# Matmul with layer norm: later row tiles of A loaded one at a time, four rows to a partition

## The chip, the cores and the metric

The kernel runs on one core of a Trainium2 chip. The metric is the device time of one execution in microseconds, and lower is better. The engines are TensorE (PE in the profile), VectorE (DVE), ScalarE (ACT), GpSimd (POOL) and SyncE (SP). SyncE, ScalarE and GpSimd also issue DMA transfers, each on a queue of its own.

## The reference

```python
m, k, n = 2048, 2048, 2048        # a: m x k, b: k x n, all float32
x = np.matmul(a, b)
mean = np.mean(x, axis=-1, keepdims=True)
var = np.var(x, axis=-1, keepdims=True)
normalized = (x - mean) / np.sqrt(var + eps)
return (gamma * normalized + beta).astype(np.float32)
```

## The kernel before

A has 16 row tiles of 128 rows (`i` or `g`), the contraction has 16 slices of 128 (`t` or `kt`), and the output has 4 column blocks of 512 (`q`), one PSUM bank each; there are 8 banks. B is loaded in 32 pieces of 512 KB, `w{kt}_{h}` with `h` 0 for the left 1024 columns and 1 for the right, through 8 buffers (`bigp`), and cast to fp16 into `b16`, where all of it stays. Each piece is cast half by VectorE and half by ScalarE (`cast_left`, `cast_right`). A matmul needs A transposed, `at[i]`, with the contraction in the partitions. The order of every engine's instructions is the order in which the code is written; each engine works through its own list, and semaphores between them are set by the tiles that they share.

The program has these stages:

- Tiles 0 to 3 of A are loaded by the sixteen `f` loads, cast by VectorE and transposed by TensorE. Tiles 0 to 3 are multiplied with B in four phases: left half with slices 0 to 7, right half with slices 0 to 7 (their sums are put by in SBUF), left half with slices 8 to 15, right half with slices 8 to 15. At the end of each of the last two phases `add_up` adds the sum put by and so frees the bank, and `stats` takes row statistics.
- Tiles 4 to 15 then run one after the other, each with all of B: 4 blocks of 16 matmuls. During tile `i` VectorE takes the statistics of its blocks, transposes tile `i + 2`, and normalises tile `i - 1` and, up to tile 11, a half of one of the tiles 0 to 3. `centre` is the first step of `normalise`; it reads the bank, and behind it the bank can be used by the second tile after.
- Tile 15 is normalised by three engines at the end (`normalise_last`).

The later tiles of A, 4 to 15, are loaded in pieces of 512 KB named `p`, through 4 buffers (`firstp`, shared with the `f` loads). A load is four DMAs, one for each group `q` of 32 partitions. ScalarE casts the piece to fp16 (6 buffers, `a16p`). VectorE's transpose then turns blocks of 32 by 32, each within 32 partitions. So the group `q` of 32 partitions has to hold the contraction columns that `at` wants in those partitions, and the four groups come from four places of the contraction. Contraction column `512 c + 128 q + 4 s + t` goes to partition `32 q + s`, slice `4 c + t`, in A as in B.

Before the change a piece `p{i}_{c}` belongs to a pair of tiles, `i` and `i + 1`: partition `32 q + r` holds the rows `r`, `32 + r`, ... of both tiles (eight rows) with one quarter `c` of the contraction. Its first four rows are tile `i`, its last four tile `i + 1`. All four pieces are needed for the first of the two tiles. The pieces of the pair 4, 5 are issued on SyncE's queue, one after each second load of B's last eight; the other pairs on GpSimd's queue:

```python
for t in range(KH, n_kt):
    load_b(t, 1)
    if t % 2:
        load_pair(4, (t - KH) // 2, nc.sync)
```

SyncE's queue ends its inputs with gamma and beta, broadcast to all partitions. The outputs follow on it.

Of the kernel before, what the change touches and what calls it, by code (L numbers as in the profile page):

```python
# [9 lines left out]
FP32 = mybir.dt.float32  # L10
FP16 = mybir.dt.float16
# [4 lines left out]
def kernel(  # L16
# [9 lines left out]
    nc = tc.nc  # L26
    P = 128
    M, K = a.shape
    _, N = b.shape
    n_mt = M // P  # L30
    n_kt = K // P
# [8 lines left out]
    firstp = ctx.enter_context(tc.tile_pool(name="firstp", bufs=4))  # L40
    first16 = ctx.enter_context(tc.tile_pool(name="first16", bufs=2))
    a16p = ctx.enter_context(tc.tile_pool(name="a16p", bufs=6))
# [11 lines left out]
    b16 = bpool.tile([P, n_kt, N], FP16)  # L54

    b_rows = b.rearrange("(c p t) n -> c t p n", p=P, t=4)
    a_pieces = a.rearrange("(s r) (c q k) -> q c r s k", r=32, c=4, q=4)

    bnst, x_of, mv_of, rs_of, at = {}, {}, {}, {}, {}
    a_in, b_in, t_of, pair_in, part = {}, {}, {}, {}, {}  # L60

    def load_b(kt, h, queue=None):
        w = bigp.tile([P, NH], FP32, tag="big", name=f"w{kt}_{h}")
# [8 lines left out]
    def cast_right(kt):  # L72
        w = b_in.pop((kt, 1))
        nc.vector.tensor_copy(b16[:, kt, NH:NH + NB], w[:, 0:NB])  # L74
        nc.scalar.copy(b16[:, kt, NH + NB:N], w[:, NB:NH])
# [3 lines left out]
    def load_first(n):  # L79
        g, c = pieces[n]  # L80
        f = firstp.tile([P, 4 * P], FP32, tag="first", name=f"f{g}_{c}")
        nc.sync.dma_start(f, a[ts(g, P), ts(c, 4 * P)])
        a_in[n] = f
# [12 lines left out]
        g, c = pieces[n]  # L96
        nc.vector.tensor_copy(at[g][:, ds(4 * c, 4), :], t_of[n])

    def load_pair(i, c, queue):
        f = firstp.tile([P, 8, P], FP32, tag="first", name=f"p{i}_{c}")  # L100
        for q in range(4):
            queue.dma_start(f[ds(32 * q, 32)], a_pieces[q, c][:, ds(4 * i, 8)])  # L102
        pair_in[i, c] = f

    def cast_pair(i, c):
        h = a16p.tile([P, 8, P], FP16, tag="a16", name=f"a{i}_{c}")
        nc.scalar.copy(h, pair_in.pop((i, c)))  # L107
        a_in["pair", i, c] = h[:, 0:4]
        a_in["pair", i + 1, c] = h[:, 4:8]

    def new_at(i):
        at[i] = atp.tile([P, n_kt, P], FP16, tag="at", name=f"at{i}")

    def transpose_part(i, c):
        nc.vector.transpose(
            at[i][:, ds(4 * c, 4), :].rearrange("p t (j r) -> p j t r", r=32),
            a_in["pair", i, c].rearrange("p j (k t) -> p j t k", t=4),
        )

    def bank(i, q):  # L120
# [8 lines left out]
    def stats(i, q):  # L129
        if i not in bnst:  # L130
            bnst[i] = stat.tile([P, n_nb, 6], FP32, tag="bnst", name=f"bnst{i}")
        nc.vector.bn_stats(bnst[i][:, q, :], x_of[i, q])
# [78 lines left out]
    with tc.manual_schedule(engines=order):  # L211
        nc.vector.memset(warm, 0.0)  # L212
        nc.vector.memset(ident, 0.0)
        nc.vector.memset(eps_t, float(eps))
        w_ps = psum.tile([P, NB], FP32, tag="c_ps", bufs=8, name="w_ps")

        def warm_up(n):
            for _ in range(n):
                nc.tensor.matmul(w_ps, warm[:, 0:P], warm, start=True, stop=True)  # L219

        nc.gpsimd.affine_select(
            out=ident, in_=ident, compare_op=AluOp.not_equal, fill=1.0,
            base=0, pattern=[[-1, P]], channel_multiplier=1,
        )
        KH = n_kt // 2
        load_first(0)
        load_b(0, 0, nc.scalar)
        load_first(1)
        for n in range(1, KH):
            load_first(n + 1)  # L230
            load_b(n, 0)
        for t in range(KH):
            load_b(t, 1)
            if KH + t + 1 < n_kt:
                load_first(KH + t + 1)
        for t in range(KH, n_kt):
            load_b(t, 0)
        for t in range(KH, n_kt):
            load_b(t, 1)
            if t % 2:  # L240
                load_pair(4, (t - KH) // 2, nc.sync)
        nc.sync.dma_start(gamma_b, gamma.unsqueeze(0).to_broadcast([P, N]))
        nc.sync.dma_start(beta_b, beta.unsqueeze(0).to_broadcast([P, N]))
        for i in range(6, n_mt, 2):
            for c in range(4):
                load_pair(i, c, nc.gpsimd)

        left = [(g, q) for g in range(G) for q in (0, 1)]
        right = [(g, q) for g in range(G) for q in (2, 3)]
        early, late = left[:-1], left[-1]  # L250
        for g in range(G):
            new_at(g)

        warm_up(10)
        cast_first(0)
        turn_first(0)
        cast_first(1)
        warm_up(2)
        for n in range(KH):
            g, c = pieces[n]  # L260
            keep_first(n)
            cast_left(n)
            cast_first(n + 2)
            if n + 1 < KH:
                turn_first(n + 1)
            if n in (0, 1, 2):
                warm_up((3, 3, 2)[n])
            if c == 0:
                for x in early:
                    if x[0] == g:  # L270
                        bank(*x)
            if n == KH - 1:
                break
            for t in range(g + 1):
                for gg, q in early:
                    if gg <= g and (gg == g or t == g):
                        mm(gg, q, 4 * c + t, 0, KH)
        bank(*late)
        cast_right(0)
        for g, q in early:  # L280
            for t in range(4 if g == 3 else KH - 1, KH):
                mm(g, q, t, 0, KH)
            put_by(g, q)
            if (g, q) == (1, 1):
                cast_right(1)
        for t in range(KH):
            mm(*late, t, 0, KH)
        cast_right(2)
        put_by(*late)

        early, late = right[:-1], right[-1]
        for g, q in early:
            bank(g, q)
        for t in range(KH):
            n = KH + t
            turn_first(n)
            if t > 2:
                cast_right(t)
            keep_first(n)
            if n + 2 < n_kt:  # L300
                cast_first(n + 2)
            if t < KH - 2:
                for g, q in early:
                    mm(g, q, t, 0, KH)
        bank(*late)
        for t in range(KH, KH + 2):
            cast_left(t)
        for g, q in early:
            for t in (KH - 2, KH - 1):
                mm(g, q, t, 0, KH)  # L310
            put_by(g, q)
        for t in range(KH):
            mm(*late, t, 0, KH)
        put_by(*late)
        for t in range(KH + 2, n_kt):
            cast_left(t)

        for g, q in left:
            bank(g, q)
        for t in range(KH, KH + 3):  # L320
            for g, q in left:
                mm(g, q, t, KH)
        for j, (g, q) in enumerate(left):
            for t in range(KH + 3, n_kt):
                mm(g, q, t, KH)
            add_up(g, q)
            if j % 3 == 2:
                cast_right(KH + j // 3)

        for g, q in right:  # L330
            bank(g, q)
        new_at(4)
        for c in range(4):
            for t in (KH + 2 * c, KH + 2 * c + 1):
                if t > KH + 1:
                    cast_right(t)
            for g, q in left[4 * c:4 * c + 4]:
                stats(g, q)
            cast_pair(4, c)
            if c < 3:  # L340
                transpose_part(4, c)
        for t in range(KH, n_kt - 2):
            for g, q in right:
                mm(g, q, t, KH)
        for j, (g, q) in enumerate(right):
            for t in (n_kt - 2, n_kt - 1):
                mm(g, q, t, KH)
            add_up(g, q)
            if j == 2:
                transpose_part(4, 3)  # L350
        for g, q in right:
            stats(g, q)
        new_at(5)
        for c in range(4):
            transpose_part(5, c)
            cast_pair(6, c)

        for i in range(G, n_mt):
            if i > G:
                normalise(i - 1)  # L360
            if i + 2 < n_mt:
                new_at(i + 2)
            for q in range(n_nb):
                bank(i, q)
                for t in range(n_kt):
                    mm(i, q, t)
                stats(i, q)
                if i + 2 < n_mt:
                    transpose_part(i + 2, q)
                if i % 2 and i + 3 < n_mt:  # L370
                    cast_pair(i + 3, q)
                if q == 3 and i < 3 * G:
                    normalise((i - G) // 2, (i - G) % 2)
        normalise_last(n_mt - 1)
# [31 lines left out]
```

## Time and profile before

| | us |
|---|---|
| median of 6 runs | 261.87 |
| lowest, highest | 258.91, 264.14 |
| the profiled execution, its own time | 263.12 |
| its span, first to last instruction | 261.3 |
| TensorE busy in the span | 236.9 (91%) |
| VectorE busy | 193.6 (74%) |
| ScalarE busy | 59.0 (23%) |
| GpSimd busy | 49.5 (19%) |

The profile is of one execution. Its own time is 1.8 us longer than the span, since it also holds what lies before the first and behind the last instruction. All times within the trace count from the start of the span. In a timeline a row is: start, duration, engine, line, operation, output and inputs, count, and in brackets how long the engine had been idle and what ended that. A matmul's duration is modelled and overlaps the next one's; the distance of two starts is what it costs. `q` behind an engine's name means its queue: `SPq` is SyncE issuing DMAs. Buffer numbers are left out of names there, so `p_1_196` is a piece `p{i}_1`, and `ps_2_781` a bank of block 2.

### The profile page before, as it was taken

What the parts mean: (1) busy time and instruction counts of PE and PEld (TensorE: products, weight loads), DVE (VectorE), ACT (ScalarE), POOL (GpSimd) and SP (SyncE); (2) the same over time, 40 slices, a digit from 0 to 9 for tenths busy, and PEclk for the clock granted to TensorE, in tenths of its full rate; (3) what the DMA queues carried; (4) which work ended last, traced back from release to release, by engine and by line L of the source; (5) the groups of instructions that cost most, each with busy time, mean ns of one, the idle gap of its engine ahead of it and who ended that gap; (6) DMA issues with size and microseconds to landing.
All of it is one profiled execution on the core that took longest, in us unless ns stands there. A gap on an engine that the chain in (4) does not pass through costs nothing.

```text
span 261.3 us, 3106 instructions
## 1 busy us (share of the span) xinstructions
PE 236.9 (91%) x1108; PEld 107.0 (41%) x1108; DVE 193.6 (74%) x354; ACT 59.0 (23%) x91; POOL 49.5 (19%) x87
## 2 busy tenths in 40 slices
PE   7998989998618999999999999999999999999950
PEld 2454444443202444444444444444444444444420
DVE  1663454379215997999899989999999988665553
ACT  2235617533224150330033003300330000000010
POOL 0000000003313582770055203730000000000003
PEclk9999999999995999999999999999999999999995
DMA  6999999999999765796159712983142303030304
GB/s 203 401 382 404 383 351 413 290 223 244 253 241 278 170 164 106 235 278 224 70 199 268 258 80 110 301 233 161 80 163 82 161 14 149 0 161 0 161 0 161
DMA packets 20303, 52.62 MB, mean 201 GB/s; under 512 B 2881, under 2 KB 6977, under 8 KB 20033
## 3 DMA queue, kind: packets, MB, share of 16 engines
q1 hardware_dynamic: 16160, 41.16, 45.8%
q0 software_dynamic: 3840, 10.49, 17.1%
q10 hardware_dynamic: 288, 0.79, 0.9%
q8 instruction: 8, 0.13, 0.2%
q14 instruction: 7, 0.05, 0.1%
HBM read 35.65 MB, written 16.78 MB: 201 GB/s over the span
## 4 chain that ended last, share of the span: by engine, by line
PE 67%; DMA 26%; DVE 3%; issue 1%; SPq 1%; ACT 0%; ACTq 0%; DVEq 0%
DMA w_1_212<-in_b_dram 5%; DMA p_0_187<-in_a_dram 4%; DMA w_0_173<-in_b_dram 4%; DMA w_1_145<-in_b_dram 4%; DMA p_1_196<-in_a_dram 3%; DMA f_1_129<-in_a_dram 3%; DMA f_0_113<-in_a_dram 3%; PE ps_3_2189 L124 1%; PE ps_0_2134 L124 1%; PE ps_1_2058 L124 1%; PE ps_2_1979 L124 1%; PE ps_3_1898 L124 1%; PE ps_0_1840 L124 1%; PE ps_1_1746 L124 1%; PE ps_2_1649 L124 1%; PE ps_3_1558 L124 1%
## 5 line engine op out<-in xcount | busy, mean ns | idle before, releaser
L197 POOL TENSOR_TENSOR y_last<-y_last,gamma_b 128x512 f32<-128x512 f32 x1 | 1.3, 1266 | 81.9 <-ACT y_last L196 81.9
L102 POOL DMA_DIRECT2D p_0_221<-in_a_dram x4 | 2.5, 626 | 57.3 <-DMA p_1_196<-in_a_dram 57.3
L124 PEld LDWEIGHTS <-at_321 128*128 128x128 f16 x64 | 6.0, 99 | 17.6 <-issue 12.9
L124 PE MATMUL ps_2_781<-b_93,at_321 128*128 128x512 f16 x8 | 3.4, 430 | 9.6 <-DVE b_93 L74 9.6
L124 PEld LDWEIGHTS <-at_323 128*128 128x128 f16 x64 | 6.4, 101 | 8.4 <-issue 1.8
L124 PEld LDWEIGHTS <-at_324 128*128 128x128 f16 x64 | 6.4, 100 | 8.3 <-issue 1.6
L124 PEld LDWEIGHTS <-at_322 128*128 128x128 f16 x64 | 6.4, 101 | 8.0 <-issue 1.1
L124 PEld LDWEIGHTS <-at_919 128*128 128x128 f16 x64 | 6.3, 98 | 7.5
L124 PEld LDWEIGHTS <-at_1033 128*128 128x128 f16 x64 | 6.3, 98 | 7.5
L124 PEld LDWEIGHTS <-at_1379 128*128 128x128 f16 x64 | 6.3, 98 | 7.5
L124 PEld LDWEIGHTS <-at_1493 128*128 128x128 f16 x64 | 6.3, 98 | 7.5
L124 PEld LDWEIGHTS <-at_1839 128*128 128x128 f16 x64 | 6.3, 98 | 7.5
L124 PEld LDWEIGHTS <-at_1939 128*128 128x128 f16 x64 | 6.3, 98 | 7.5
L124 PEld LDWEIGHTS <-at_1263 128*128 128x128 f16 x64 | 6.3, 98 | 7.5
L124 PEld LDWEIGHTS <-at_1723 128*128 128x128 f16 x64 | 6.3, 98 | 7.5
L124 PEld LDWEIGHTS <-at_906 128*128 128x128 f16 x64 | 6.3, 98 | 7.5
L124 PEld LDWEIGHTS <-at_789 128*128 128x128 f16 x64 | 6.2, 97 | 7.6
L124 PEld LDWEIGHTS <-at_1149 128*128 128x128 f16 x64 | 6.2, 97 | 7.6
L124 PEld LDWEIGHTS <-at_1609 128*128 128x128 f16 x64 | 6.2, 97 | 7.6
L219 PE MATMUL w_ps<-warm 128*128 128x512 f16 x20 | 7.3, 505 | 1.2 <-DVE warm L212 1.2
L102 POOL DMA_DIRECT2D p_0_281<-in_a_dram x4 | 2.3, 584 | 15.9 <-ACT a_0_1284 L107 15.9
L102 POOL DMA_DIRECT2D p_0_301<-in_a_dram x4 | 2.3, 584 | 15.5 <-ACT a_0_1514 L107 15.5
(580 smaller groups left out, 593.0 us busy)
## 6 DMA issues: line engine op xcount, KB each, us to landing
gamma_b<-in_gamma_dram SPq DMA_DIRECT2D x1, 1024.0 KB, 14.5
beta_b<-in_beta_dram SPq DMA_DIRECT2D x1, 1024.0 KB, 16.0
w_0_105<-in_b_dram ACTq DMA_DIRECT2D x1, 512.0 KB, 5.2
w_0_111<-in_b_dram SPq DMA_DIRECT2D x1, 512.0 KB, 7.0
w_0_115<-in_b_dram SPq DMA_DIRECT2D x1, 512.0 KB, 7.8
w_0_119<-in_b_dram SPq DMA_DIRECT2D x1, 512.0 KB, 6.4
w_0_123<-in_b_dram SPq DMA_DIRECT2D x1, 512.0 KB, 7.0
w_0_127<-in_b_dram SPq DMA_DIRECT2D x1, 512.0 KB, 7.8
```

Source lines behind the costliest of these rows:

```text
L102: queue.dma_start(f[ds(32 * q, 32)], a_pieces[q, c][:, ds(4 * i, 8)])
L124: nc.tensor.matmul(x_of[i, q], at[i][:, kt, :], b16[:, kt, ds(q * NB, NB)], start=(kt == lo), stop=(kt == hi - 1),)
L197: nc.gpsimd.tensor_tensor(y, y, gamma_b[:, q3], AluOp.mult)
L219: nc.tensor.matmul(w_ps, warm[:, 0:P], warm, start=True, stop=True)
```

## The change

A piece `p{i}_{h}` now belongs to one tile and one half `h` of its rows. Partition `32 q + r` holds the four consecutive rows `4 r` to `4 r + 3` of the tile, two of them in each half, with all four quarters of the contraction. The size is the same, 512 KB, and so are the four DMAs of 32 partitions and their runs of 512 bytes; a tile needs two pieces. A transpose now takes row `j` of each partition with the whole contraction, 16 slices by 32 rows, and writes every fourth column of `at[i]`, from column `j` on. Before, it took four rows of a partition with four slices and wrote all columns of these.

```diff
-    a_pieces = a.rearrange("(s r) (c q k) -> q c r s k", r=32, c=4, q=4)
+    a_pieces = a.rearrange("(i r j) (c q k) -> q i r (j c) k", r=32, j=4, c=4, q=4)
...
-    def load_pair(i, c, queue):
-        f = firstp.tile([P, 8, P], FP32, tag="first", name=f"p{i}_{c}")
+    def load_tile(i, h, queue):
+        f = firstp.tile([P, 8, P], FP32, tag="first", name=f"p{i}_{h}")
         for q in range(4):
-            queue.dma_start(f[ds(32 * q, 32)], a_pieces[q, c][:, ds(4 * i, 8)])
-        pair_in[i, c] = f
-
-    def cast_pair(i, c):
-        h = a16p.tile([P, 8, P], FP16, tag="a16", name=f"a{i}_{c}")
-        nc.scalar.copy(h, pair_in.pop((i, c)))
-        a_in["pair", i, c] = h[:, 0:4]
-        a_in["pair", i + 1, c] = h[:, 4:8]
+            queue.dma_start(f[ds(32 * q, 32)], a_pieces[q, i][:, ds(8 * h, 8)])
+        tile_in[i, h] = f
+
+    def cast_tile(i, h):
+        a16 = a16p.tile([P, 2, 4, P], FP16, tag="a16", name=f"a{i}_{h}")
+        nc.scalar.copy(a16.rearrange("p j c k -> p (j c) k"), tile_in.pop((i, h)))
+        tile_in[i, h] = a16
...
-    def transpose_part(i, c):
+    def transpose_part(i, j):
         nc.vector.transpose(
-            at[i][:, ds(4 * c, 4), :].rearrange("p t (j r) -> p j t r", r=32),
-            a_in["pair", i, c].rearrange("p j (k t) -> p j t k", t=4),
+            at[i].rearrange("p ct (r j) -> p j ct r", j=4)[:, j],
+            tile_in[i, j // 2][:, j % 2].rearrange("p c (k t) -> p c t k", t=4),
         )
...
-            if t % 2:
-                load_pair(4, (t - KH) // 2, nc.sync)
+        for i in (4, 5):
+            for h in (0, 1):
+                load_tile(i, h, nc.sync)
...
-        for i in range(6, n_mt, 2):
-            for c in range(4):
-                load_pair(i, c, nc.gpsimd)
+        for i in range(6, n_mt):
+            for h in (0, 1):
+                load_tile(i, h, nc.gpsimd)
```

The hand-written order around the change moves with it: the casts of B's right half now stand between the add-ups of the left half and between its statistics, tile 4's casts and transposes stand behind all of them, and from tile 6 on each tile's two casts stand in the loop of the tile two before it, where the four casts of a pair stood in every second tile's loop.

On SyncE's queue, in B's last eight right halves and what follows (`w{kt}_1` is a right half of B, `p4_0` the first piece of tile 4, or of the pair 4 and 5), there stood before:

```order
L64 DMA w9_1_185<-in_b_dram 128x1024
L102 DMA p4_0_187<-in_a_dram 32x8x128 x4
L64 DMA w10_1_192<-in_b_dram 128x1024
L64 DMA w11_1_194<-in_b_dram 128x1024
L102 DMA p4_1_196<-in_a_dram 32x8x128 x4
L64 DMA w12_1_201<-in_b_dram 128x1024
L64 DMA w13_1_203<-in_b_dram 128x1024
L102 DMA p4_2_205<-in_a_dram 32x8x128 x4
L64 DMA w14_1_210<-in_b_dram 128x1024
L64 DMA w15_1_212<-in_b_dram 128x1024
L102 DMA p4_3_214<-in_a_dram 32x8x128 x4
L242 DMA gamma_b_88<-in_gamma_dram 128x2048
```

and in the changed kernel, in the same place:

```order
L64 DMA w10_1_187<-in_b_dram 128x1024
L64 DMA w11_1_189<-in_b_dram 128x1024
L64 DMA w12_1_191<-in_b_dram 128x1024
L64 DMA w13_1_193<-in_b_dram 128x1024
L64 DMA w14_1_195<-in_b_dram 128x1024
L64 DMA w15_1_197<-in_b_dram 128x1024
L102 DMA p4_0_199<-in_a_dram 32x8x128 x4
L102 DMA p4_1_204<-in_a_dram 32x8x128 x4
L102 DMA p5_0_209<-in_a_dram 32x8x128 x4
L102 DMA p5_1_214<-in_a_dram 32x8x128 x4
L242 DMA gamma_b_88<-in_gamma_dram 128x2048
```

The four loads of A moved behind the last load of B; their number is the same.

On VectorE, behind the add-ups of the left half (`x_2_0` is the sum of tile 2, block 0, `b16` the cast B, `at4` tile 4 transposed), there stood before:

```order
L115 STREAM_TRANSPOSE at4_789<-a4_1_809 128x4x4x32
L74 CAST b16_93<-w12_1_201 128x512
L74 CAST b16_93<-w13_1_203 128x512
L115 STREAM_TRANSPOSE at4_789<-a4_2_816 128x4x4x32
L74 CAST b16_93<-w14_1_210 128x512
L74 CAST b16_93<-w15_1_212 128x512
L140 TENSOR_TENSOR x_0_2_649<-ps_0_2_781,x_0_2_649 128x512
L140 TENSOR_TENSOR x_0_3_653<-ps_0_3_782,x_0_3_653 128x512
L140 TENSOR_TENSOR x_1_2_657<-ps_1_2_783,x_1_2_657 128x512
L115 STREAM_TRANSPOSE at4_789<-a4_3_823 128x4x4x32
L140 TENSOR_TENSOR x_1_3_661<-ps_1_3_784,x_1_3_661 128x512
```

and in the changed kernel:

```order
L74 CAST b16_93<-w15_1_197 128x512
L131 BN_STATS bnst2_807<-x_2_0_500 128x6
L131 BN_STATS bnst2_807<-x_2_1_503 128x6
L131 BN_STATS bnst3_810<-x_3_0_509 128x6
L131 BN_STATS bnst3_810<-x_3_1_521 128x6
L114 STREAM_TRANSPOSE at4_861<-a4_0_862 128x512 x2
L114 STREAM_TRANSPOSE at4_861<-a4_1_866 128x512 x2
L139 TENSOR_TENSOR x_0_2_649<-ps_0_2_783,x_0_2_649 128x512
L139 TENSOR_TENSOR x_0_3_653<-ps_0_3_784,x_0_3_653 128x512
```

All casts of B now stand ahead of tile 4's four transposes, and these together stand ahead of the add-ups of the right half.

More of the change, by code (lines that the diff above doesn't have):

```diff
@@ L56 @@
     b_rows = b.rearrange("(c p t) n -> c t p n", p=P, t=4)
-    a_pieces = a.rearrange("(s r) (c q k) -> q c r s k", r=32, c=4, q=4)
+    a_pieces = a.rearrange("(i r j) (c q k) -> q i r (j c) k", r=32, j=4, c=4, q=4)
     bnst, x_of, mv_of, rs_of, at = {}, {}, {}, {}, {}
-    a_in, b_in, t_of, pair_in, part = {}, {}, {}, {}, {}
+    a_in, b_in, t_of, tile_in, part = {}, {}, {}, {}, {}
     def load_b(kt, h, queue=None):
@@ L326 @@
             add_up(g, q)
-            if j % 3 == 2:
-                cast_right(KH + j // 3)
+            if j % 2 and j < 6:
+                cast_right(KH + j // 2)
         for g, q in right:
             bank(g, q)
[L332 to L341, printed above, removed]
+        for t in range(KH + 3, n_kt):
+            cast_right(t)
+            stats(*left[t - KH - 3])
+        for g, q in left[5:]:
+            stats(g, q)
         for t in range(KH, n_kt - 2):
@@ L344 @@
                 mm(g, q, t, KH)
-        for j, (g, q) in enumerate(right):
+        new_at(4)
+        for h in (0, 1):
+            cast_tile(4, h)
+            transpose_part(4, 2 * h)
+            transpose_part(4, 2 * h + 1)
+        for g, q in right:
             for t in (n_kt - 2, n_kt - 1):
@@ L348 @@
             add_up(g, q)
-            if j == 2:
-                transpose_part(4, 3)
         for g, q in right:
@@ L354 @@
         for c in range(4):
+            if c % 2 == 0:
+                cast_tile(5, c // 2)
             transpose_part(5, c)
-            cast_pair(6, c)
         for i in range(G, n_mt):
@@ L368 @@
                 if i + 2 < n_mt:
+                    if q % 2 == 0:
+                        cast_tile(i + 2, q // 2)
                     transpose_part(i + 2, q)
-                if i % 2 and i + 3 < n_mt:
-                    cast_pair(i + 3, q)
                 if q == 3 and i < 3 * G:
```

## The prediction, made before the changed kernel was run

> **What bounds the kernel now.** I read the page first: the span, TensorE's row in forty slices of 6.5 us, and the clock granted to it.
>
> ```profile
> span 261.3 us, 3106 instructions
> ...
> PE   7998989998618999999999999999999999999950
> ...
> PEclk9999999999995999999999999999999999999995
> ```
>
> TensorE is dense except at the start, in the last two slices, and from the tenth to the twelfth (59 to 78 us), where its row reads 8, 6, 1. The thirteenth has a granted clock of 5 tenths. The chain that ended last says what TensorE was waiting for there (columns: start us, us, what).
>
> ```profile
> 65.43 14.00 DMA w_1_212<-in_b_dram
> ...
> 79.45 0.45 DVE b_93 L74
> ...
> 85.90 3.45 PE ps_0_920 L124 x16
> ...
> 113.53 3.45 PE ps_0_1150 L124 x16
> ...
> 248.21 3.47 PE ps_3_2189 L124 x16
> ```
>
> The last half row of B (`w_1_212`, k-slice 15, right half) landed at 79.4, VectorE cast it, and from 85.90 (tile 4) to 251.68 TensorE ran without a break at 3.45 / 16 = 0.2158 us a matmul. 9.7 us of tail follow. So from 85.90 on the time belongs to TensorE, and every microsecond by which tile 4 starts sooner is a microsecond of the span, as long as VectorE and the loads keep up. TensorE's timeline shows the phase ahead of tile 4, the right half of tiles 0 to 3:
>
> ```profile
> 58.78 0.38 PE L124 MATMUL ps_2_781<-b_93,at_321 128*128 128x512 f16 x1
> ...
> 63.09 0.38 PE L124 MATMUL ps_2_781<-b_93,at_321 128*128 128x512 f16 x1 [0.70 <-DVE b_93 L74]
> ...
> 67.84 0.38 PE L124 MATMUL ps_2_781<-b_93,at_321 128*128 128x512 f16 x1 [1.13 <-DVE b_93 L74]
> ...
> 71.15 0.38 PE L124 MATMUL ps_2_781<-b_93,at_321 128*128 128x512 f16 x1 [1.42 <-DVE b_93 L74]
> ...
> 78.40 0.59 PE L124 MATMUL ps_2_781<-b_93,at_321 128*128 128x512 f16 x1 [5.37 <-DVE b_93 L74]
> 79.95 0.59 PE L124 MATMUL ps_2_781<-b_93,at_321 128*128 128x512 f16 x1 [0.96 <-DVE b_93 L74]
> ```
>
> The phase takes 85.90 - 58.78 = 27.12 us. It holds 64 matmuls (8 banks by 8 k-slices), 64 x 0.2158 = 13.81 us. The excess is 13.31 us: 9.58 us of idle time in five waits for casts of B, and 3.7 us of slow matmuls and resumptions. The windows of one microsecond show the slow ones (busy, count, granted clock, DMA share, GB/s):
>
> ```profile
> 72.00:73.00 1.00, 1.00 (x5) 1.00 1.15 209
> ...
> 79.00:80.00 1.00, 0.05 (x1) 0.50 1.07 274
> ```
>
> By these rows the clock is still full behind the waits of 0.70 to 1.42 us and halved behind the one of 5.37 us.
>
> **Why B is late.** VectorE's casts of B's left half show the rate of B alone, ScalarE's casts the landings after that, and SyncE's timeline the issues.
>
> ```profile
> 40.62 0.43 DVE L69 CAST b_93<-w_0_167 128x512 f16<-128x512 f32 x1 [0.32 <-DMA w_0_167<-in_b_dram]
> ...
> 48.30 0.43 DVE L69 CAST b_93<-w_0_179 128x512 f16<-128x512 f32 x1 [0.85 <-DMA w_0_179<-in_b_dram]
> ```
>
> ```profile
> 50.23 0.62 ACT L70 CAST b_93<-w_0_181 128x512 f16<-128x512 f32 x1 [1.22 <-DMA w_0_181<-in_b_dram]
> ...
> 70.67 0.62 ACT L75 CAST b_93<-w_1_203 128x512 f16<-128x512 f32 x1 [2.69 <-DMA w_1_203<-in_b_dram]
> 75.85 1.04 ACT L107 CAST a_2_816<-p_2_205 128x1024 f16<-128x1024 f32 x1 [4.57 <-DMA p_3_214<-in_a_dram]
> ...
> 79.45 0.62 ACT L75 CAST b_93<-w_1_212 128x512 f16<-128x512 f32 x1 [0.92 <-DMA w_1_212<-in_b_dram]
> ```
>
> ```profile
> 52.72 3.62 SPq L102 DMA_DIRECT2D p_1_196<-in_a_dram  x4
> 56.85 0.35 SPq L64 DMA_DIRECT2D w_1_201<-in_b_dram  x1
> ...
> 65.43 0.37 SPq L64 DMA_DIRECT2D w_1_212<-in_b_dram  x1
> ```
>
> Six loads of B land in 48.30 - 40.62 = 7.68 us, 1.28 us each. From 50.23 to 79.45, 29.2 us, come 8 loads of B, 8 x 1.28 = 10.2 us, and beside them three loads of A on SyncE's queue and two on GpSimd's. The 19.0 us left make 3.8 us for each load of A, though it has B's size (512 KB). It also blocks SyncE for 3.62 us where a load of B takes 0.35. GpSimd's two are released by the casts of the first two loads of A:
>
> ```profile
> 58.90 2.48 POOL L102 DMA_DIRECT2D p_0_221<-in_a_dram  x4 [57.32 <-DMA p_1_196<-in_a_dram]
> ...
> 94.89 2.31 POOL L102 DMA_DIRECT2D p_2_251<-in_a_dram  x4
> 97.19 2.31 POOL L102 DMA_DIRECT2D p_3_256<-in_a_dram  x4
> ```
>
> **The change, part by part.** (1) *B without A between.* SyncE issues B's last eight halves in a row, and since tile 6 reuses the buffer of tile 4's first half, GpSimd's loads start behind that half's cast. So neither kind stands in front of B: it lands by 50.23 + 8 x 1.28 = 60.5 instead of 79.4. Its casts follow the add-ups of the left half on VectorE:
>
> ```profile
> 59.05 0.69 DVE L140 TENSOR_TENSOR x_1_521<-ps_1_704,x_1_521 128x512 f32<-128x512 f32 x1 [0.39 <-PE ps_1_704 L124]
> ...
> 92.75 0.67 DVE L115 STREAM_TRANSPOSE at_906<-a_1_809 128x512 f16<-128x512 f16 x1
> 93.34 0.67 DVE L115 STREAM_TRANSPOSE at_906<-a_2_816 128x512 f16<-128x512 f16 x1
> ...
> 101.24 0.75 DVE L157 SCALAR_TENSOR_TENSOR u_0_1002<-x_0_486,mv_997,gamma_b 128x512 f32<-128x512 f32 x1
> ...
> 104.25 0.75 DVE L157 SCALAR_TENSOR_TENSOR u_0_1016<-ps_0_920,mv_1011,gamma_b 128x512 f32<-128x512 f32 x1
> ...
> 141.19 0.70 DVE L132 BATCH_NORM_STATS2 bnst_1281<-ps_3_1328 128x6 f32<-128x512 f32 x1 [0.28 <-PE ps_3_1328 L124]
> ...
> 155.00 0.70 DVE L132 BATCH_NORM_STATS2 bnst_1397<-ps_3_1438 128x6 f32<-128x512 f32 x1 [0.64 <-PE ps_3_1438 L124]
> ```
>
> The last add-up ends at 59.74. Five casts (0.43) and four statistics (0.70) put k-slice 15 in place by 64.7, and TensorE asks for it behind 48 matmuls, at 58.78 + 10.36 = 69.1. Even B at half its rate (70.7) would be barely late. So the right phase runs gapless from 58.78 to 58.78 + 13.81 = 72.6: **13.3 us** gained, the slow clock included.
>
> (2) *Tile 4 behind B.* Two loads instead of four, but now behind B, and the first matmul of the tile needs all four transposes, since each fills every fourth column. Two loads at 3.8 from 60.5 land at 68.1, the cast takes 1.04, two transposes at a pitch of 93.34 - 92.75 = 0.59 end at 70.3. VectorE is free before that (eight statistics and five casts after 59.74 end by 67.5). The add-ups of the right half stand behind these transposes; the first frees tile 4's bank at 70.3 + 0.69 = 71.0. Both are ready ahead of 72.6. Bounds for one load of A: 2.30 us (GpSimd's issue pitch, 97.19 - 94.89) and 5.2 us (75.85 - 70.67, with GpSimd's load beside it). At 5.2 the loads land at 70.9 and the bank is free at 73.8, 1.2 us late. I take 3.8, nothing lost.
>
> (3) *VectorE's order.* The eight right add-ups now end near 70.3 + 8 x 0.69 = 75.8, 3.2 us into tile 4. The limit is a bank: `centre` gave tile 4's first bank back at 105.00 and tile 6 took it at 113.53, 8.5 us of room. No cost.
>
> (4) *Gamma and beta* stay at the end of SyncE's input queue:
>
> ```profile
> 75.80 0.35 SPq L243 DMA_DIRECT2D beta_b<-in_beta_dram  x1
> ...
> beta_b<-in_beta_dram SPq DMA_DIRECT2D x1, 1024.0 KB, 16.0
> ```
>
> Beta landed at 91.8. If it comes no sooner, the first `centre` (101.24 - 13.3 = 87.9) is followed by a wait of at most 3.9 us on VectorE, inside the 8.5. No cost.
>
> (5) *The transposes.* There are 48 before and after, of 512 elements each, and 24 loads and 24 casts of the same size. New is that results are written to every fourth 2-byte element. No row shows such a write. The nearest row is the same transpose, which already reads at that step at a pitch of 0.59 us, so I take +0. The other end is one more cycle an element: the pitch doubles, +0.59. A saving is excluded, since neither elements nor instructions become fewer. The Trainium skill, page "SBUF — State Buffer", section "Door 1: The DMA port swizzle", says that a 16-byte line needs two accesses to run at full rate; at a step of 8 bytes there are exactly two, so by that rule the write is free and the sum stays, and at one access it would not. No row here shows such a write.
>
> Sum on the profiled execution, 263.12 us: 263.12 - 13.3 = 249.8. The median of the six runs is 261.87, 1.25 us lower, which gives 248.6. I say **249.0**.
>
> **Rivals.** *Tile 4's loads take the place of B's.* TensorE would wait at 72.6 for the last transpose instead. For it: the fifth wait before was 5.37 us, with loads of A in front. Against it: the margin of 2.3 us above. The bounds give 0 to 1.2 us; if SyncE's blocking adds its 3.62 us once, 4.8 us: 250 to 255. By the rows above the clock is halved somewhere between a wait of 1.42 and one of 5.37 us, and it cost 3.7 us; with that again, 258. The Trainium skill, page "TensorE: Matmul & The Clock Gate", section "What's actually happening", puts that point at an idle window of about 3.4 us; by that rule the 4.8 us would end at 258, and the trace agrees as far as its two rows go.
>
> *Strided writes make VectorE the bound.* In tiles 4 to 11 VectorE idles only 0.28 and 0.64 us a tile in turn. With d more for a transpose it falls behind by 4d - 0.46 a tile, for 8 tiles, and 8.5 us are tolerated. At d = 0.59: 8 x 1.90 - 8.5 = 6.7 us, and tile 4's transposes use up the margin: 256.5. At d = 1.18: 8 x 4.26 - 8.5 = 25.6, plus 4.7 - 2.3 at tile 4: 278, **slower than before**. It decides from 36d - 3.7 - 8.5 - 2.3 = 13.3, d = 0.77 us, a transpose of more than twice its pitch. Against it is the reading side at the same step.
>
> *The loads are not what holds B.* If the eight buffers' release set B's pace, B would still end near 79 us: 261, no change. Against it: 1.28 us a load through the same buffers up to 48.30, and `w_1_201` issued only behind `p_1_196`.
>
> **How the numbers follow.** Forecast (248 to 251) 0.70; tile 4 late (250 to 258) 0.13; transposes at two cycles (256.5) 0.06; slower transposes (over 265) 0.04; B only partly relieved (252 to 262) 0.05; no change 0.02. A measurement of this kernel tells about 1% from no change, 2.6 us. The range 247 to 257 leaves out about 0.1, the slow transposes and a B hardly relieved; it takes in the bounds of loads and writes. Faster by over 1% 0.91, within 1% 0.04, slower 0.05.
>
> **What would show it.** The last half of B should land near 60 us and TensorE start tile 4 near 72.6 with granted clock 1.0 throughout, no wait over 1 us between 59 and 73; transposes should stay at 0.67 to 0.71 us; TensorE's 166 us behind tile 4's start should stay, and the tail 9.7 us. I am wrong if transposes are longer, if a wait for `at` opens at 72 us, or if B's loads keep a pace over 2 us each without A.

## The result, and the profile after

The changed kernel took 252.96 us (median of 10 runs, 252.01 to 254.32). The kernel before took 262.46 us in 20 runs. The ratio is 0.9705, with a 95% interval of 0.9667 to 0.9744: 3% faster. The forecast was 249.0 us, most likely 248 to 251, in a range of 247 to 257. The direction and the larger term were right, and 4 us of the forecast gain did not come.

The page of the changed kernel, in the rows that the prediction began with:

```profile
span 251.2 us, 3093 instructions
...
PE   7999999999999999999999999989979899999940
...
PEclk9999999999999999999999999999999999999995
```

The hole from 59 to 78 us is gone, and so is the half clock behind it. New are small dents in the 27th to the 32nd slice (163 to 201 us), where before there was none. Part 4 of the page, the shares of the chain that ended last, for the kernel before and then for the changed one:

```profile
PE 67%; DMA 26%; DVE 3%; issue 1%; SPq 1%; ACT 0%; ACTq 0%; DVEq 0%
```

```profile
DVE 56%; PE 22%; DMA 15%; issue 3%; ACT 2%; SPq 0%; DVEq 0%
```

Before, the chain went through TensorE and the loads. Now more than half of it is VectorE. TensorE's timeline of the changed kernel shows both effects:

```profile
57.60 0.38 PE L123 MATMUL ps_2_783<-b_93,at_321 128*128 128x512 f16 x1
...
71.41 3.62 PE L123 MATMUL ps_0_912<-b_93,at_861 128*128 128x512 f16 x16
...
85.23 3.62 PE L123 MATMUL ps_0_1030<-b_93,at_902 128*128 128x512 f16 x16
...
154.75 3.61 PE L123 MATMUL ps_0_1602<-b_93,at_1371 128*128 128x512 f16 x16 [0.29 <-DVE u_0_1472 L156]
...
169.68 3.61 PE L123 MATMUL ps_0_1720<-b_93,at_1489 128*128 128x512 f16 x16 [0.96 <-DVE u_0_1584 L156]
...
185.01 3.61 PE L123 MATMUL ps_0_1832<-b_93,at_1601 128*128 128x512 f16 x16 [1.35 <-DVE u_0_1702 L156]
...
199.95 3.61 PE L123 MATMUL ps_0_1936<-b_93,at_1719 128*128 128x512 f16 x16 [0.97 <-DVE u_0_1814 L156]
```

The same view of the kernel before has the start of its tile 4:

```profile
85.74 3.62 PE L124 MATMUL ps_0_920<-b_93,at_789 128*128 128x512 f16 x16
```

The right half of tiles 0 to 3 takes 71.41 - 57.60 = 13.81 us where it took 85.74 - 58.78 = 26.96: 13.15 us gained. (The prediction's 85.90 is from the chain, which puts this start 0.16 us later than the timeline.) The phase also began 1.18 us sooner than in the profile before (57.60 against 58.78). That lead is already there at 42 us, ahead of the first load that moved (issued at 43.17 before), so it does not belong to the change. At the first blocks of tiles 10 to 13 TensorE waits for `centre` (line 156) of the tile two before it, which has to give the bank back. From tile 4 to its last matmul TensorE takes 170.1 us instead of 165.9. The four waits are 3.6 us of these 4.2; by the distance of the starts each costs some 0.16 us more than its idle time. So 261.3 - 13.15 - 1.18 + 4.2 = 251.2, the span.

ScalarE's casts show that the loads came as forecast, or sooner:

```profile
60.61 0.62 ACT L75 CAST b_93<-w_1_197 128x512 f16<-128x512 f32 x1 [1.14 <-DMA w_1_197<-in_b_dram]
63.02 1.05 ACT L107 CAST a_0_862<-p_0_199 128x1024 f16<-128x1024 f32 x1 [1.79 <-DMA p_0_199<-in_a_dram]
64.97 1.05 ACT L107 CAST a_1_866<-p_1_204 128x1024 f16<-128x1024 f32 x1 [0.91 <-DMA p_1_204<-in_a_dram]
67.54 1.05 ACT L107 CAST a_0_903<-p_0_209 128x1024 f16<-128x1024 f32 x1 [1.52 <-DMA p_0_209<-in_a_dram]
71.66 1.05 ACT L107 CAST a_1_907<-p_1_214 128x1024 f16<-128x1024 f32 x1 [3.08 <-DMA p_1_214<-in_a_dram]
```

VectorE's timeline has what the experiments below show to be the cause of the new waits: a transpose takes 1.3 us instead of 0.7.

```profile
64.91 2.46 DVE L114 STREAM_TRANSPOSE at_861<-a_0_862 128x512 f16<-128x512 f16 x2
67.17 2.51 DVE L114 STREAM_TRANSPOSE at_861<-a_1_866 128x512 f16<-128x512 f16 x2
69.46 0.74 DVE L139 TENSOR_TENSOR x_2_649<-ps_2_783,x_2_649 128x512 f32<-128x512 f32 x1
...
73.68 0.70 DVE L139 TENSOR_TENSOR x_3_683<-ps_3_790,x_3_683 128x512 f32<-128x512 f32 x1
...
84.10 1.31 DVE L114 STREAM_TRANSPOSE at_911<-a_0_931 128x512 f16<-128x512 f16 x1
85.20 0.65 DVE L131 BATCH_NORM_STATS2 bnst_929<-ps_1_934 128x6 f32<-128x512 f32 x1
85.75 1.32 DVE L114 STREAM_TRANSPOSE at_911<-a_0_931 128x512 f16<-128x512 f16 x1
...
88.52 0.65 DVE L131 BATCH_NORM_STATS2 bnst_929<-ps_3_974 128x6 f32<-128x512 f32 x1
```

The same place in the kernel before, a transpose and the next one with a row of statistics between:

```profile
95.11 0.68 DVE L115 STREAM_TRANSPOSE at_919<-a_0_908 128x512 f16<-128x512 f16 x1
...
96.31 0.68 DVE L115 STREAM_TRANSPOSE at_919<-a_1_911 128x512 f16<-128x512 f16 x1
```

Back to back, a transpose now costs (67.17 - 64.91) / 2 = 1.13 us, where it cost 0.59. With statistics between, a pair costs 85.75 - 84.10 = 1.65 instead of 96.31 - 95.11 = 1.20, so 0.45 more.

### The profile page after: what moved, and what is told of

The parts are those of the page before. It is cut to its first block, busy times and chain, and to the rows that moved or that the text cites. A ratio compares the mean times of both kernels' runs of the same rounds, so it can differ in the third digit from the quotient of the medians.

```text
span 251.2 us, 3093 instructions
## 1 busy us (share of the span) xinstructions
PE 235.0 (94%) x1108; PEld 106.9 (43%) x1108; DVE 214.0 (85%) x354; ACT 58.2 (23%) x91; POOL 49.4 (20%) x87
## 4 chain that ended last, share of the span: by engine, by line
DVE 56%; PE 22%; DMA 15%; issue 3%; ACT 2%; SPq 0%; DVEq 0%
DMA w_0_169<-in_b_dram 4%; DMA w_1_137<-in_b_dram 4%; DMA w_1_153<-in_b_dram 3%; DMA f_1_121<-in_a_dram 2%; DMA f_0_107<-in_a_dram 2%; DVE at_911 L114 2%; DVE at_1719 L114 2%; DVE at_1489 L114 2%; DVE at_1259 L114 2%; DVE at_1601 L114 2%; DVE at_1141 L114 2%; DVE at_1371 L114 2%; DVE at_1029 L114 2%; DVE at_861 L114 2%; DVE at_902 L114 2%
## 5 line engine op out<-in xcount | busy, mean ns | idle before, releaser
L102 POOL DMA_DIRECT2D p_0_221<-in_a_dram x4 | 2.5, 626 | 62.8 <-DMA p_0_209<-in_a_dram 62.8
L218 PE MATMUL w_ps<-warm 128*128 128x512 f16 x20 | 8.4, 568 | 1.2 <-DVE warm L211 1.2
L123 PE MATMUL ps_0_1832<-b_93,at_1601 128*128 128x512 f16 x16 | 3.6, 378 | 1.4 <-DVE u_0_1702 L156 1.4
L123 PE MATMUL ps_0_1936<-b_93,at_1719 128*128 128x512 f16 x16 | 3.6, 378 | 1.0 <-DVE u_0_1814 L156 1.0
L123 PE MATMUL ps_0_1720<-b_93,at_1489 128*128 128x512 f16 x16 | 3.6, 379 | 1.0 <-DVE u_0_1584 L156 1.0
```

Of the source, the lines that this page charges most:

```text
L102: queue.dma_start(f[ds(32 * q, 32)], a_pieces[q, i][:, ds(8 * h, 8)])
L123: nc.tensor.matmul(x_of[i, q], at[i][:, kt, :], b16[:, kt, ds(q * NB, NB)], start=(kt == lo), stop=(kt == hi - 1),)
```

## The experiments

Two theories stood against each other. The first: the gain is the order of the loads, and the loss is the write step of the transposes. The second: the transposes or VectorE are late for another reason that came with the new order (later landings, per-tile casts, add-ups behind the transposes).

### The new order with the old pieces

The kernel before, with the pair's four pieces behind B and the casts in the changed order:

```diff
         for t in range(KH, n_kt):
             load_b(t, 1)
-            if t % 2:
-                load_pair(4, (t - KH) // 2, nc.sync)
+        for c in range(4):
+            load_pair(4, c, nc.sync)
```

> The new order of loads and casts with the old pieces and the old transposes: all four pieces of the pair 4 and 5 stand behind B. If the strided write is what costs (first theory): transposes at a pitch of 0.59 us, tile 4 starts at 71 to 73 us, no wait of TensorE behind it, 248 to 250 us. Its fourth piece lands near 72 and is wanted at 74 (slice 12 of the first block), so up to 1 us may be lost there. If VectorE is late because of the new order or the later landings (second theory): the waits of 4 us in tiles 10 to 13 stay and the time is 252 to 254 us. If B's early landing were not what brought the gain, 262 us.

It took 249.09 us; the ratio to the kernel before is 0.9511 (0.9446 to 0.9575). In its chain TensorE stands as one piece, 889 matmuls to the last one:

```profile
44.21 192.05 PE ps L124 x889
```

The order alone brings the whole gain, and without the strided write nothing is lost again. Whether B waited before for the transfers of A themselves or for SyncE, which each load of A held for 3.1 to 5.0 us, the runs do not separate. The fourth piece, on which this version depends, was cast at 69.86 and transposed at 70.94 (ScalarE's and VectorE's timelines), ahead of its use:

```profile
69.86 1.04 ACT L107 CAST a<-p 128x1024 f16<-128x1024 f32 x1 [2.29 <-DMA p<-in_a_dram]
```

```profile
70.94 0.71 DVE L115 STREAM_TRANSPOSE at<-a 128x512 f16<-128x512 f16 x1 [0.85 <-ACT a L107]
```

### The new pieces in the old order

The changed kernel, with its first four loads of A and their casts between those of B as before:

```diff
             load_b(t, 1)
-        for i in (4, 5):
-            for h in (0, 1):
-                load_tile(i, h, nc.sync)
+            if t % 2:
+                n = (t - KH) // 2
+                load_tile(4 + n // 2, n % 2, nc.sync)
```

> The new pieces and the strided transposes with the loads in the old places, between those of B. First theory: tile 4 starts near 85 us as before the change, transposes take 1.3 us, VectorE falls behind by 1.4 us a tile and TensorE waits 2 to 5 us in tiles 10 to 13: 264 to 267 us, slower than before the change. Second theory: 261 to 263 us, no wait in the later tiles.

It took 264.52 us, with a ratio of 1.0122 (1.0072 to 1.0173): 1.2% slower than the kernel before. One of its ten executions took 508.93 us, for a reason that is not known; the median hardly feels it. Its waits of TensorE (us in total, times, longest) show the old loss and the new one side by side:

```profile
PE ps L123 <- DVE b L74: 9.7, 4, 4.5
PE ps L123 <- DVE u L156: 2.1, 2, 1.1
```

So the two halves of the change have opposite signs, and each keeps its sign without the other. The waits for `centre` are shorter than in the changed kernel (2.1 us against 3.6). Tile 4 is transposed there while TensorE waits for B anyway, so VectorE goes into the later tiles less far behind: the statistics of tile 4's last block start at 99.97, about 1.5 us behind the block's matmuls (an estimate: their end, some 98.4, is counted back from tile 12 at 0.2158 us a matmul), where the changed kernel is 3.3 us behind.

### Contiguous writes, rows put back by the output's DMAs

The changed kernel, in which tiles 4 to 13 keep the order of their load; a store is four DMAs of 32 rows:

```diff
+        if mixed(i):                       # tiles 4 to 13
+            o = at[i][:, :, ds(32 * j, 32)]
...
+        rows = out[ts(i, P), cols].rearrange("(r j) n -> j r n", j=4)
+        for j in range(4):
+            nc.sync.dma_start(rows[j], c[ds(32 * j, 32)])
```

> The change with contiguous writes of the transposes for tiles 4 to 13: the rows stay in the order of the load, and the output's DMAs put them back (four DMAs of 32 rows each in place of one of 128). Tiles 14 and 15 keep the strided write, where VectorE has room. First theory: transposes of tiles 4 to 13 at a pitch of 0.59 us, no wait of TensorE from tile 4 on, 248 to 250 us, if sixteen instead of four output DMAs a pair of tiles do not hold up the c buffers (then a wait of VectorE for a DMA would show). Second theory: 252 to 254 us.

It took 248.61 us, with a ratio of 0.9504 (0.9444 to 0.9564). Its chain has one piece of 918 matmuls; no wait for `centre` is among TensorE's waits:

```profile
38.88 198.15 PE ps L137 x918
```

This refutes the second theory. Loads, casts, reads and the order of VectorE's instructions are those of the change; only the places of the results and the output's DMAs differ. Tiles 14 and 15 still write at the wide step in this version, and that costs TensorE nothing.

### Steps of writing and reading

One kernel with a different write and read step in each tile:

> The change with other steps in the transposes of tiles 6 to 15, same 512 elements: the columns of the transposed tiles land in other places, so the output of these tiles is not the reference's; only the durations count. Write step, read step in elements of 2 bytes: tile 6: 1, 4; 7: 2, 4; 8: 4, 4; 9: 8, 4; 10: 4, 1; 11: 1, 1; 12: 2, 1; 13: 8, 1; 14: 16, 4; 15: 1, 4. First theory, write alone counts: 0.7 us wherever the write step is 1 and 1.3 at 4, whatever the read step. If one access to an 8-byte unit is what costs, step 2 still takes 0.7; if every step but 1 costs, step 2 takes 1.3; if 16-byte lines count on top, steps 8 and 16 take more than 1.3. Rival: both steps together cost, then tile 10 takes 0.7.

VectorE's timeline, the first of the four transposes of each tile, tiles 6 to 15 in order:

```profile
84.77 0.71 DVE L131 STREAM_TRANSPOSE at<-a 128x512 f16<-128x512 f16 x1
...
98.20 0.73 DVE L131 STREAM_TRANSPOSE at<-a 128x512 f16<-128x512 f16 x1
...
111.30 1.30 DVE L131 STREAM_TRANSPOSE at<-a 128x512 f16<-128x512 f16 x1
...
126.60 2.44 DVE L131 STREAM_TRANSPOSE at<-a 128x512 f16<-128x512 f16 x1
...
145.56 1.30 DVE L131 STREAM_TRANSPOSE at<-a 128x512 f16<-128x512 f16 x1
...
160.86 0.69 DVE L131 STREAM_TRANSPOSE at<-a 128x512 f16<-128x512 f16 x1
...
173.91 0.73 DVE L131 STREAM_TRANSPOSE at<-a 128x512 f16<-128x512 f16 x1
...
187.36 2.44 DVE L131 STREAM_TRANSPOSE at<-a 128x512 f16<-128x512 f16 x1
...
206.31 2.32 DVE L131 STREAM_TRANSPOSE at<-a 128x512 f16<-128x512 f16 x1
...
222.23 0.69 DVE L131 STREAM_TRANSPOSE at<-a 128x512 f16<-128x512 f16 x1
```

By write step in elements: 1 takes 0.69 to 0.71 us, 2 takes 0.73, 4 takes 1.30, 8 takes 2.44, 16 takes 2.32. The read step does not matter: at write step 4 it is 1.30 for a read step of 4 (tile 8) and of 1 (tile 10), at write step 8 it is 2.44 both times (tiles 9 and 13). The rival that both steps together cost has fallen. Step 2 is as good as free, and 8 takes more than 1.3, so of the cases named beforehand the one with 16-byte lines on top is borne out.

### Two rows a partition

The probe has a step of 2 as good as free. Two consecutive rows to a partition in each half tile lead to that step. The four DMAs of a piece then cover 64 whole rows that follow each other; in the change they cover pairs of rows with pairs left out between:

```diff
-    a_pieces = a.rearrange("(i r j) (c q k) -> q i r (j c) k", r=32, j=4, c=4, q=4)
+    a_pieces = a.rearrange("(i h r s) (c q k) -> q i h r (s c) k", h=2, r=32, s=2, c=4, q=4)
...
-            at[i].rearrange("p ct (r j) -> p j ct r", j=4)[:, j],
+            at[i].rearrange("p ct (h r s) -> p h s ct r", h=2, s=2)[:, j // 2, j % 2],
```

> The change with two consecutive rows a partition instead of four in each half tile: half h holds the rows 64 h to 64 h + 63, and a transpose writes every second column of its half, a write step of 2 elements, 4 bytes. The probe had 0.72 us at that step. If the write step's cost is the whole loss: transposes at a pitch of 0.6 us, TensorE without a wait from tile 4 to the end, 248 to 250 us, the same as the permuted store. If loading a tile singly costs something of its own beside the write: above the run with the old pieces by 1 us or more.

> The new order of loads with the old pieces and transposes, beside the change itself and the two rows on one chip: 248 to 250 us, 4 us (1.5%) below the change and within 1 us of the two rows if the write step is the whole loss.

> The change itself on the same chip: 252 to 254 us, TensorE waiting 4 us in tiles 10 to 13 for VectorE.

The three ran on one chip, against the same runs of the kernel before:

| | median us | ratio to before, 95% |
|---|---|---|
| two rows a partition | 249.13 | 0.9517 (0.9465 to 0.9569) |
| new order, old pieces | 248.63 | 0.9498 (0.9448 to 0.9548) |
| the change | 253.82 | 0.9700 (0.9643 to 0.9757) |

The first two cannot be told apart. Both are some 5 us below the change, and their intervals lie below its own. TensorE's chain in the first is again one piece, while the change has its waits for `centre` (the waits of the run on the same chip):

```profile
45.57 192.05 PE ps L123 x889
```

```profile
PE ps L123 <- DVE u L156: 3.6, 4, 1.3
```

Loading a tile singly costs nothing that can be seen; the write step is the whole loss. Three versions without it end at 248.6 to 249.1 us.

### Other writers

> The two rows with one extra instruction ahead of the first transpose of each tile from 6 on; the transposes write over what it wrote, so the result stays. It moves 512 contiguous 2-byte elements to every w-th one: VectorE's copy with w of 1, 2, 4, 8 (tiles 6 to 9), ScalarE's copy with 1, 2, 4, 8 (tiles 10 to 13), VectorE's sum of two tiles with 1 and 4 (14, 15). If a write unit of 4 bytes limits every writer of SBUF: VectorE's copy and sum double from w = 2 to 4 as the transposes do, ScalarE's copy too. If it is the transpose's own drain: the copies and the sum change by less than 0.1 us from 2 to 4 (a copy may be faster at 1, where its elements can go in pairs).

VectorE's copies with write steps 1, 2, 4, 8, then its sums with 1 and 4:

```profile
81.70 0.28 DVE L135 COPY at<-a 128x512 f16<-128x512 f16 x1
...
96.42 0.45 DVE L135 COPY at<-a 128x512 f16<-128x512 f16 x1
...
110.02 0.72 DVE L135 COPY at<-a 128x512 f16<-128x512 f16 x1
...
124.26 1.29 DVE L135 COPY at<-a 128x512 f16<-128x512 f16 x1
...
192.76 0.41 DVE L139 TENSOR_TENSOR at<-a 128x512 f16<-128x512 f16 x1
...
203.93 1.29 DVE L139 TENSOR_TENSOR at<-a 128x512 f16<-128x512 f16 x1
```

ScalarE's copies with 1, 2, 4, 8:

```profile
133.99 0.62 ACT L137 COPY at<-a 128x512 f16<-128x512 f16 x1
147.46 0.77 ACT L137 COPY at<-a 128x512 f16<-128x512 f16 x1
160.57 1.35 ACT L137 COPY at<-a 128x512 f16<-128x512 f16 x1
174.61 2.49 ACT L137 COPY at<-a 128x512 f16<-128x512 f16 x1
```

It is not the transpose's own drain: ScalarE's copy goes up by the same steps, VectorE's sum takes as long as a transpose at step 4, and VectorE's copy takes about half of it at the steps 4 and 8. From 2 to 4 the copies go up by 0.58 and 0.27 us; neither doubles as the first expectation had it.

## Why the prediction was right, and where it was not

**B without A between: right.** B's last half was cast at 60.61 (forecast 60.5), the right phase took 13.81 us without a wait, and the clock stayed full. The gain came in full: 13.15 us by the timeline, forecast 13.3. The runs confirm it from the other side: with A back between B's loads, 9.7 us of waiting return.

**Tile 4 behind B: right, with one term too large.** A load of A behind B landed 63.02 - 60.61 = 2.4, 1.95, 2.6 and 4.1 us after the one before, 2.8 on average where I took 3.8. The second, the last that tile 4 needs, was there 3.1 us ahead of the forecast (64.97 against 68.1). The slower transposes used most of that up: the last one of tile 4 ended at 69.7, forecast 70.3, against a start at 71.41.

**VectorE's order, gamma and beta: right.** The add-ups ended 3.0 us into tile 4 (forecast 3.2), and no wait for gamma or beta opened.

**The transposes: wrong, and this is the step that failed.** I took +0 for the write at every fourth element, because the same instruction already reads at that step at full rate. Reading was the wrong neighbour: the probe shows that the read step costs nothing and the write step doubles the instruction. Bounding it by a doubled pitch was right (+0.54 us back to back against a bound of +0.59), and the rival built on it named the place, VectorE in tiles 4 to 11, and the mechanism, banks that come back late. I gave it 6 in 100. For the +0 I had also leaned on the Trainium skill, page "SBUF — State Buffer", section "Door 1: The DMA port swizzle", that two accesses to a 16-byte line suffice. For these writes the measurement disagrees: at a step of 8 bytes, two to a line, the transpose takes 1.30 us instead of 0.70.

**The price of that rival was too high**, 6.7 us for 4.2 measured, by two errors of opposite sign. Next to the statistics a transpose costs only 0.45 more, so VectorE falls behind by 4 x 0.45 - 0.46 = 1.34 us a tile. But the room of 8.5 us was counted for a VectorE that is on time. In the changed kernel the statistics of tile 4's last block start at 88.52, 3.3 us after the block's matmuls at 85.23, so 5.2 us are left for tiles 5 to 11: 7 x 1.34 - 5.2 = 4.2 us. With the 1.5 us of the new pieces in the old order the same sum gives 7 x 1.34 - 7.0 = 2.4 us, beside waits of 2.1 there.

**That the range held is in part luck.** The interval given 70 in 100, 248 to 251, did not come true. The range reached to 257 because it took in the bounds for late loads and for slow writes, and of these only the second happened. The other two rivals whose intervals hold 253, tile 4 late and B only partly relieved, did not happen.

**The clock** stayed full behind the new waits, none of which is over 1.35 us. Two other runs narrow the point at which it is halved. TensorE's timeline of the new pieces in the old order, and the window behind (its last three figures are clock, DMA share and GB/s):

```profile
63.84 3.61 PE L123 MATMUL ps<-b,at 128*128 128x512 f16 x16 [2.38 <-DVE b L74]
...
77.30 0.58 PE L123 MATMUL ps<-b,at 128*128 128x512 f16 x1 [4.54 <-DVE b L74]
```

```profile
79.00:80.00 1.00, 1.00 (x3) 0.40 (x3) 0.38 (x1) 0.14 (x1) 0.00 (x0) 0.50 1.04 356
```

Behind 2.38 us of idling sixteen matmuls still run at full rate (3.61 us), behind 4.54 us the clock is 0.50. In the probe of steps TensorE idles 3.85 us, from 197.31 to 201.16, and a window of TensorE alone shows the clock falling within that wait:

```profile
200.00:201.00 1.00, 0.00 (x0) 0.59 0.00 0
```

It is 1.00 up to 200.1 there and 0.50 from 200.2 on, so it fell after 2.9 us of idling; in the wait of 4.54 us it fell at 77.0, after 4.3 us, and in the 5.37 us of the kernel before at 78.3, after 5.3 us. No single length of a wait fits all three. The 3.4 us of the Trainium skill, page "TensorE: Matmul & The Clock Gate", section "What's actually happening", lie between the shortest and the longest of them.

## What to carry to other kernels

A change that moves a cost to another engine has to be priced at that engine's margin: VectorE had 0.28 to 0.64 us a tile to spare and was given 1.8 more. Two edits that come together should be tried apart, since here the order of the loads was worth 13 us and the layout beside it cost 4 to 5 of them, and either a narrower step or the old pieces kept the first without the second. When a strided operand is priced from a row, the row must have the stride on the same side, reading or writing.

## What the runs showed of the hardware

The write step costs transposes, VectorE's copies and sums and ScalarE's copies time, by one rule. From step 4 to 8 a 512-element transpose gains 2.44 - 1.30 = 1.14 us and ScalarE's copy 2.49 - 1.35 = 1.14; from 2 to 4 they gain 0.57 and 0.58; VectorE's copy gains half of that, 0.57 and 0.27. Beyond 8 nothing is added (2.32 at 16). From step 2 on, all of it fits an estimate of 4.45 ns (half for VectorE's copy) each time a unit of 16 bytes of a partition is touched: 1.14 us is 256 such units more, 0.57 us is 128 more, and from 16 bytes a step on every element has a unit of its own. VectorE's sum agrees (0.88 us more at step 4 than at 1, for 192 units, 0.85 by the estimate). Four 2-byte elements to a unit then pass at the rate of a transpose (0.69 us at step 1, 0.73 at step 2), and two do not. That the unit is 16 bytes rests on the rise up to a step of 8 elements and its end there, with one step (16) tried beyond. Why VectorE's copy pays half was not tried, nor were elements of 4 bytes or read steps over 4.
